# Four recurrent heads in one set of score groups, joint norms, gates ahead of the attentions, no transposes of empty causal blocks, and a planner without its shift table

## The chip, the cores and the metric

The kernel runs on one core of one Trainium2 chip. A core has TensorE (PE, 128 x 128 matrix engine, whose weight loads are shown as PEld), VectorE (DVE), ScalarE (ACT) and GpSimd (POOL), and queues that issue DMAs from SyncE (SP), ScalarE and GpSimd. The metric is device time in microseconds: the median of several executions.

## The reference

One layer of a hybrid decoder on x of 512 x 1024 in float32. Three groups read the same normed input and are merged by one output projection; a SwiGLU feed-forward layer follows. Cut to what the change touches:

```python
# A) latent attention, 4 heads, causal over blocks of 128 queries
q = (rmsnorm(c_q, q_a_norm) @ w_uq); kv = rmsnorm(c_kv, kv_a_norm) @ w_ukv
q = rmsnorm(q); k = rmsnorm(k); rope on 64 of 192 columns
p = softmax(where(kpos <= qpos, q @ k.T * scale, -inf));  o = p @ v
# B) HGRN2, 4 heads, one gated linear recurrence each
f = lb + (1 - lb) * sigmoid(f_raw); k = 1 - f; decay = exp of the cumulated log f
a[t, s] = sum_d q[t, d] * k[s, d] * decay(t, s, d)   for s <= t
o = a @ v + (carried state);  o = rmsnorm(o per head) * silu(g_raw)
# C) cross attention of 4 heads into 256 memory tokens, q and k rmsnormed
# then: x += concat(rmsnorm(A), B, rmsnorm(C)) @ w_out
#       x += (silu(h @ w_gate) * (h @ w_up)) @ w_down,  h = rmsnorm(x)
```

## The kernel before

**Arithmetic.** Every float32 operand of a large product is split into two parts, `hi` and `lo` (`split`: a cast on ScalarE, a subtraction on VectorE), and a product is three matmuls, hi·hi, hi·lo and lo·hi (`mm3`). Activations lie transposed: 128 features on the partitions, the 512 positions along the row. The feed-forward layer is a seven-product scheme (`fast`) and isn't touched.

**Order.** The program is first recorded. `run` (L244) then simulates the five engines with a price for each operation (`price`, L184), and always takes the ready operation with the least priority number; `issue` (L368) writes the instructions in that planned order, so nearly all of them carry line 388, and the matmuls of a `tiles` group (many small matmuls into column tiles of the PE array, one after the other) line 385. `rec.first(n)` gives a priority class. `NUDGE` (L242) is a table of 17 shifts of the priorities of stretches of the recording. Tiles come from rings (`BUFS`, L432): 3 PSUM banks for `mm`, 3 for `at`, 2 for `tr`; a tile waits until its ring has a free one.

**Start.** `WARM` matmuls on ones run while the first data come. ScalarE's queue issues five loads of `we` (two blocks of input weights that are needed first, `EARLY`, L402), SP's queue eight loads of x (`tm<-in_xT`), then the rest. x is split with its gain into `xh`, `xl`. The squares of x are summed (ScalarE squares, VectorE adds, `td`), `colsums` (L544) sums over the partitions with 32-wide column tiles against ones, `rsqrt_col` (L529) takes an inverse square root in ten small VectorE operations, and `spread` (L554) transposes its four columns to a 128 x 512 block, which ScalarE copies to `RX`. Each projection's bank (`mm`) is multiplied by `RX` on its way out (`td<-mm,RX`).

**Recurrence.** `hg_in` (L698) makes q, k and the gate of a head. `hg_levels` (L757) builds the causal matrix of two heads by doubling: at level m = 1, 2, ..., 64, pairs of blocks of m positions are combined. At each level a group of score matmuls (L385, `at<-y,tm`) reads the present q (`y`) and k (`tm`); for m up to 16 each head gives 16 parts of 32 x 32, spread over four column tiles; at m = 32 a head gives 8 parts; at m = 64 it gives 4 parts of 64 x 64, all in the lower column tile. `put` copies what a level has added under a mask (`cc<-lmask,at`), and `step_up` (L816) multiplies half of q and half of k by the totals of the neighbour block, in place, so that the next level's scores wait for it. Heads 0 and 1 go first, then heads 2 and 3. `hg_out` (L828) multiplies with the values and takes each head's norm by itself: a sum over partitions, an inverse root, four transposes.

**The rest.** `wide` projects the values of the recurrence (`wva` 320 columns, `wvb` 256). `lowrank` (L906) projects the compressed q and kv, each with a norm (`rcq`, `rckv`). In the attention, `softmax` makes weights `p` block by block (`p` is cleared beyond the diagonal), `weights_t` (L1062) transposes four 128 x 128 blocks of two query blocks, and `pv` (L743) multiplies with the values. `rope_t` (L1082) transposes a head's rotary part twice over into one 128 x 512 block. `hg_final` (L852) projects the output gate of a recurrent head and applies it; it is written after the latent attention. `group_norm` (L1072) norms a group's four heads jointly; that of the memory group stands right ahead of the last third of the output projection, on which the norm of the feed-forward layer rests.

Of the kernel before, what the change touches and what calls it, by code (L numbers as in the profile page):

```python
# [24 lines left out]
EPS = 1e-6  # L25
LEVELS = (1, 2, 4, 8, 16)
# [19 lines left out]
class Recorder:  # L46
# [137 lines left out]
    def price(self, o, outs, ins):  # L184
# [3 lines left out]
        if o.eng == "tensor":  # L188
            if o.name == "tiles":
                return 310 + 1.81 * sum(max(35, self._free(p[2])) for p in o.kw["parts"]) / len({self._rng(p[0])[2] for p in o.kw["parts"]})  # L190
# [50 lines left out]

    NUDGE = ((2868, 2885, -117), (1571, 1576, -1459), (2382, 2422, -477), (1732, 1734, 30), (826, 835, 186), (957, 1012, 3), (5620, 5660, 284), (3804, 3864, -113), (987, 1017, 110), (2666, 2693, -105), (2466, 2475, -61), (2533, 2540, 37), (2401, 2403, -37), (3367, 3411, -5), (3019, 3021, 346), (16, 18, 380), (2, 19, 3),)  # L242
# [158 lines left out]
WARM = 12  # L401
EARLY = {0: (1, "p"), 1: (2, "p"), 3: (2, "tc"), 5: (2, "tc"), 7: (1, "tc")}  # L402
XLAG = 0
X_ORDER = (0, 4, 1, 5, 2, 6, 3, 7)
# [8 lines left out]
def body(ctx, tc, t):  # L413
# [115 lines left out]
    def rsqrt_col(v, n):  # L529

        y = small(n)
        u = small(n)
        V.tensor_scalar(y.bitcast(I32), v.bitcast(I32), -0.5, float(0x5F3759DF), ALU.mult, ALU.add)
# [10 lines left out]
    def colsums(sqs, nblk=NB):  # L544
# [4 lines left out]
            (v[g:g + 32, i, b], sqs[i][:, b * P + g:b * P + g + 32], ones, (i, b) == ks[0], (i, b) == ks[-1])  # L549
            for i, b in ks for g in range(0, P, 32)  # L550
        ])
        return v[..., 0]
# [8 lines left out]
    def rms(sq, n):  # L561
        v = small(NB)
        V.tensor_scalar(v, colsum(sq, NB), 1.0 / n, EPS, ALU.mult, ALU.add)
# [16 lines left out]
    with rec.first(0):  # L580
# [5 lines left out]
        for k, (n, tag) in EARLY.items():  # L586
            w = ws[k] = sb(tag)[:, :2 * n * P + 8 * (k == 0)]
            A.dma_start(out=w, in_=t["we"][:, 2 * k * P + 8 * (k > 0):2 * (k + n) * P + 8])
# [3 lines left out]
        for k in range(KD):  # L592
# [5 lines left out]
            r = sb("tm")  # L598
            DMA.dma_start(out=r, in_=t["xT"][:, k * S:(k + 1) * S])
# [31 lines left out]
    early_tr[0] = False  # L631

# [65 lines left out]
    def hg_in(h):  # L698
        with rec.first(2):
            z, s_ = gated(5 + h)  # L700
            q = sb("tm")
# [3 lines left out]
            fg = sb("tm")  # L705
# [37 lines left out]
    def pv(v, h, pt, ns, y):  # L743
# [3 lines left out]
        for s in range(ns):  # L747
            mm3(o, cut(v[s], slice(None), hs), tuple(x[:, 2 * s:2 * s + 2, :].rearrange("p a b -> p (a b)") for x in pt), s == 0, s == ns - 1)
# [8 lines left out]
    def hg_levels(hs):  # L757

        N2 = range(len(hs))
        As = [sb("p", (P, NB, P)) for i in N2]  # L760
        C = sb("cc", (P, len(hs), NB, 32))
        old, hs = hs, [(sb("y"), k_, tot) for q, k_, tot in hs]

        def scores(sets):

            n = len(sets) * len(hs)
            o = ps_at()[:, 0:n * NB * 32].rearrange("p (n b t) -> p n b t", t=32, b=NB)
            ps_ = [(b, g) for b in range(NB) for g in range(0, P, 32)]
            all_ = [(i * len(hs) + j, h) for j in N2 for i, s in enumerate(sets) for h in (s[j],)]
            T.tiles(o, *[x for i, h in all_ for x in h[:2]], parts=[  # L770
# [722 lines left out]
```

## Time and profile before

| | us |
|---|---|
| median of 3 runs | 708.37 (707.99 to 708.49) |
| the profiled execution | 707.76 |
| its span, first to last instruction | 706.0 |
| TensorE busy | 697.1 (99%) |
| VectorE busy | 552.4 (78%) |
| ScalarE busy | 384.8 (55%) |
| GpSimd busy | 93.4 (13%) |

The granted TensorE clock of the span is 1.000. An instruction's duration in the trace runs from its start to its modelled end, and matmuls overlap: the distance from one start to the next is what a matmul takes of the engine. A part of a `tiles` group is two matmuls in the trace, and one in the planned order. Times are from the start of the span.

### The profile page before, as it was taken

How to read it: one execution, taken by the hardware profiler on the slowest of the kernel's cores; microseconds unless marked ns; L12 is line 12 of the kernel's file. 1: busy time of each engine (PE TensorE's matmuls, PEld its weight loads, DVE VectorE, ACT ScalarE, POOL GpSimd, SP SyncE). 2: the span in 40 equal slices, each digit the busy share in tenths (PEclk: the TensorE clock that was granted, in tenths of full speed). 3: DMA queues.
4: the chain of work that ended last, by engine and by line, in shares of the span. 5: the costliest groups of instructions: out<-in, count | busy, mean ns of one | idle time of the engine just before them, and what ended most of it. 6: DMA issues, size and time to landing. Idle time of an engine off the chain costs nothing.

```text
span 706.0 us, 13190 instructions
## 1 busy us (share of the span) xinstructions
PE 697.1 (99%) x4813; PEld 581.1 (82%) x4813; DVE 552.4 (78%) x1295; ACT 384.8 (55%) x740; POOL 93.4 (13%) x128
## 2 busy tenths in 40 slices
PE   8999999999999999999999999999999999999997
PEld 5898887787888888888788787888888899999885
DVE  5898879979978899987999969766549767448642
ACT  6653553547765686765767653645553465444320
POOL 0000100000000000000314333032113212310000
PEclk9999999999999999999999999999999999999999
DMA  8232132014511233215999999789868848941241
GB/s 285 78 95 89 64 120 66 32 62 143 185 61 61 75 94 115 77 31 161 266 250 244 221 235 229 203 175 229 190 136 187 165 124 197 218 86 30 72 145 60
DMA packets 47728, 98.05 MB, mean 139 GB/s; under 512 B 5424, under 2 KB 15536, under 8 KB 47664
## 3 DMA queue, kind: packets, MB, share of 16 engines
q1 hardware_dynamic: 33120, 73.10, 32.3%
q0 software_dynamic: 13824, 23.07, 20.5%
q10 hardware_dynamic: 720, 1.05, 0.4%
q8 instruction: 37, 0.61, 0.3%
q14 instruction: 27, 0.22, 0.1%
HBM read 95.11 MB, written 2.10 MB: 138 GB/s over the span
## 4 chain that ended last, share of the span: by engine, by line
PE 91%; DVE 5%; DMA 1%; ACT 1%; issue 1%; SPq 0%; DVEq 0%; ACTq 0%
PE mm L388 46%; PE at L388 21%; PE tr L388 21%; PE at L385 1%; DVE wl L388 1%; DVE y L388 1%; DMA tm<-in_xT 1%; DVE tm L388 1%; DVE td L388 1%; PE tr L385 1%; DMA wr<-in_wf 1%; DVE xl L388 0%; DVE hd L388 0%; DVE v L388 0%; ACT wh L388 0%
## 5 line engine op out<-in xcount | busy, mean ns | idle before, releaser
L388 ACT CAST wh<-wr 128x512 fp32r<-128x512 f32 (+2 forms) x136 | 80.7, 598 | 96.4 <-PE mm L388 49.8
L388 DVE TENSOR_TENSOR wl<-wr,wh 128x512 fp32r<-128x512 f32 (+2 forms) x148 | 96.5, 659 | 31.9 <-issue 12.2
L388 PE MATMUL mm<-xh,wh 128*128 128x512 f32 x248 | 98.1, 398 | 1.4 <-ACT xh L388 1.2
L388 PE MATMUL mm<-xh,wl 128*128 128x512 f32 x248 | 99.0, 399 | 0.4 <-DVE wl L388 0.4
L388 PE MATMUL mm<-xl,wh 128*128 128x512 f32 x248 | 98.7, 399 | 0.3 <-DVE xl L388 0.2
L388 DVE TENSOR_TENSOR wl<-y,wh 128x512 fp32r<-128x512 f32 (+1 forms) x84 | 53.3, 639 | 43.3 <-PE tr L388 17.3
L388 ACT CAST wh<-y 128x512 fp32r<-128x512 f32 (+1 forms) x81 | 46.7, 580 | 67.5 <-PE at L388 36.7
L388 DVE TENSOR_TENSOR wl<-mx,wh 128x512 fp32r<-128x512 f32 (+1 forms) x72 | 45.9, 646 | 28.8 <-PE tr L388 19.3
L388 PE MATMUL mm<-wh,hd 128*128 128x512 f32 (+2 forms) x188 | 63.9, 366 | 0.0
L388 ACT CAST wh<-mx 128x512 fp32r<-128x512 f32 (+1 forms) x67 | 39.2, 586 | 40.9 <-PE at L388 21.6
L388 PEld LDWEIGHTS mm<-xh,wh 128*128 128x128 f32 x248 | 46.5, 188 | 11.1 <-ACT xh L388 2.1
L388 PEld LDWEIGHTS mm<-xl,wh 128*128 128x128 f32 x248 | 46.6, 188 | 10.4 <-DVE xl L388 2.2
L388 PEld LDWEIGHTS mm<-xh,wl 128*128 128x128 f32 x248 | 46.7, 188 | 8.4 <-DVE wl L388 1.0
L388 PE MATMUL at<-wh,hd 128*128 128x512 f32 (+1 forms) x132 | 49.2, 375 | 0.0
L388 POOL DMA_DIRECT2D y<-in_wu x36 | 33.3, 983 | 95.8 <-DVE wl L388 76.3
L388 PE MATMUL tr<-xl,wh 128*128 128x512 f32 x112 | 43.8, 391 | 0.0
L388 PE MATMUL tr<-xh,wh 128*128 128x512 f32 x112 | 43.8, 391 | 0.0
L388 PE MATMUL tr<-xh,wl 128*128 128x512 f32 x112 | 43.7, 390 | 0.0
L388 PEld LDWEIGHTS mm<-wh,hd 128*128 128x128 f32 x188 | 34.5, 188 | 5.0 <-ACT wh L388 0.3
L388 PE MATMUL mm<-wl,hd 128*128 128x512 f32 (+2 forms) x100 | 37.0, 370 | 0.1
L388 PE MATMUL mm<-wh,v 128*128 128x512 f32 (+1 forms) x96 | 36.3, 378 | 0.0
L388 PE MATMUL at<-wh,v 128*128 128x512 f32 (+1 forms) x96 | 35.8, 375 | 0.0
(376 smaller groups left out, 1719.8 us busy)
## 6 DMA issues: line engine op xcount, KB each, us to landing
wr<-in_wf SPq DMA_DIRECT2D x19, 512.0 KB, 3.7
wr<-in_wd SPq DMA_DIRECT2D x16, 512.0 KB, 4.9
mx<-in_wg SPq DMA_DIRECT2D x24, 256.0 KB, 5.2
mx<-in_wu SPq DMA_DIRECT2D x24, 256.0 KB, 5.2
y<-in_wu POOLq DMA_DIRECT2D x24, 256.0 KB, 5.7
tm<-in_xT SPq DMA_DIRECT2D x16, 256.0 KB, 4.2
wr<-in_wt SPq DMA_DIRECT2D x8, 512.0 KB, 4.4
wr<-in_wo SPq DMA_DIRECT2D x8, 512.0 KB, 3.7
```

What stands on the lines that cost most here:

```text
L385: r = self.nc.tensor.matmul(get(a), lhsT=get(b), rhs=get(c), start=first, stop=last, skip_group_check=True)
L388: r = getattr(getattr(self.nc, o.eng), o.name)(*[get(a) for a in o.args], **{k: get(a) for k, a in o.kw.items()})
```

## The change

- `rsqrt_col` has eight small operations in place of ten (another first guess, one Newton step and one step of higher order; its input is scaled by the constant `RC`).
- `EARLY` and `WARM`: 10 warm matmuls in place of 12; three of the five loads of `we` stay on ScalarE's queue, two go to SP's, between the loads of x. `NUDGE` is gone, and the price of a `tiles` group is 270 + 2.1 per column in place of 310 + 1.81.
- `hg_in` is called for all four heads ahead of `wva` and `wvb`, q and the gate in halves of the rings `pth` and `ptl`. `hg_levels` takes four heads: each group of score parts holds all four (64 parts up to m = 16; from m = 32 on, heads 0 and 1 and heads 2 and 3 lie in different column tiles). Their matrices lie in the ring `tm`.
- `hg_out` takes no norm; `hg_norm` takes that of the four heads in one group of column sums and one inverse root over 16 columns. The two low-rank norms are joined in the same way, and stand ahead of `hg_out`.
- `hg_gate`, the projections of the output gates with their application, stands ahead of the latent attention; `hg_final` only splits.
- In the latent attention the block above the diagonal of each pair of query blocks isn't transposed: three transposes in place of four, and GpSimd clears that block of `pth` and `ptl` in place of `p`. `rope_t` takes two heads of q in one block.
- The memory group's norm sums the squares of three heads in one group and those of the fourth in a second one.

The core of the diff:

```diff
-            if o.name == "tiles":
-                return 310 + 1.81 * sum(...) / len({...})
+                return 270 + 2.1 * sum(...) / len({...})
-    NUDGE = ((2868, 2885, -117), (1571, 1576, -1459), ...
-        for a, b, d in self.NUDGE:
-            for o in ops[a:b]:
-                o.prio += d
-WARM = 12
-EARLY = {0: (1, "p"), 1: (2, "p"), 3: (2, "tc"), 5: (2, "tc"), 7: (1, "tc")}
+WARM = 10
+EARLY = {0: (1, "p"), 1: (1, "p"), 2: (2, "tc"), 4: (2, "tc"), 6: (2, "tc")}
...
-        for _ in range(3):
-            V.tensor_tensor(u, y, y, ALU.mult)
-            V.scalar_tensor_tensor(u, u, -0.5, v, ALU.mult, ALU.mult)
-            V.scalar_tensor_tensor(y, u, 1.5, y, ALU.add, ALU.mult)
+        V.tensor_tensor(u, y, y, ALU.mult)
+        V.scalar_tensor_tensor(u, u, -1.0, v, ALU.mult, ALU.mult)
+        V.scalar_tensor_tensor(y, u, 2.38924456, y, ALU.add, ALU.mult)
+        V.tensor_tensor(u, y, y, ALU.mult)
+        V.scalar_tensor_tensor(u, u, 0.703952253**2, v, ALU.mult, ALU.mult)
+        V.scalar_tensor_tensor(u, u, -10 / 3, u, ALU.add, ALU.mult)
+        V.scalar_tensor_tensor(y, u, 5.0, y, ALU.add, ALU.mult)
...
+                    (A if k < 4 else DMA).dma_start(out=w, in_=t["we"][...])
+            xin.append(sb("tm"))
+            with rec.first(-1):
+                DMA.dma_start(out=xin[k], in_=t["xT"][:, k * S:(k + 1) * S])
...
+        def scores(hs):
+            o = ps_at().rearrange("p (n b t) -> p n b t", t=32, b=NB)
+            ks = [(j, b) for j in range(HN) for b in range(NB)]
+            T.tiles(o, *[x for h in hs for x in h[:2]], parts=[
+                (o[g:g + 32, j, b], hs[j][1][:, b * P + g:b * P + g + 32], hs[j][0][:, b * P + g:b * P + g + 32], (j, b) == ks[0], (j, b) == ks[-1])
+                for j, b in ks for g in range(0, P, 32)
+            ])
...
+                w = min(m, 64)
+                T.tiles(o, *[x for h in hs for x in h[:2]], parts=[
+                    (o[i + s * m:i + (s + 1) * m, j, b], hs[2 * s + j][1][:, b * P + i:b * P + i + m], hs[2 * s + j][0][:, b * P + i + m:b * P + i + 2 * m], (j, b) == ks[0], (j, b) == ks[-1])
+                    for j, b in ks for i in at for s in range(2)
+                ])
...
-        R = spread(rms(sumsq([y], tag="tc"), P))
-        V.scalar_tensor_tensor(y, y, smc("g_hg", h), R, ALU.mult, ALU.mult)
+    def hg_norm(ys):
+        v = small(4 * NB)
+        V.tensor_scalar(v.rearrange("p (h b) -> p h b", b=NB), colsums([sumsq([y], tag=("tc", "td")[h % 2]) for h, y in enumerate(ys)]), RC / P, RC * EPS, ALU.mult, ALU.add)
+        r = rsqrt_col(v, 4 * NB)
+        for h, y in enumerate(ys):
+            V.scalar_tensor_tensor(y, y, smc("g_hg", h), spread(r[:, h * NB:(h + 1) * NB]), ALU.mult, ALU.mult)
...
-    qkf = [hg_in(0), hg_in(1)]
+    qkf = [hg_in(h) for h in range(4)]
...
-    for h, st in enumerate(hg_levels(qkf)):
-        yh.append(hg_out(h, *st))
-    qkf = [hg_in(2), hg_in(3)]
-    for h, st in enumerate(hg_levels(qkf)):
-        yh.append(hg_out(2 + h, *st))
+    qkt = hg_levels(qkf)
...
+    for h in range(4):
+        hg_gate(h, yh[h])
...
+            ends = causal and s == ns - 2
+            if ends:
+                for x in pt:
+                    G.memset(f(x)[:, 2 * s, :], 0.0)
-            for i in range(4):
+            for i in range(ends, 4):
...
-        R = spread(rms(sumsq(ys, tag="tc"), S))
+        n = 3 if late else 4
+        R = spread(rms(sumsq(ys[:n], tag="tc"), S, sumsq(ys[3:], tag="tc") if late else None))
...
-    group_norm(ys, 8, "g_mo", ("xh", "xl"))
+    group_norm(ys, 8, "g_mo", ("xh", "xl"), True)
```

**Where the order of instructions changes.** Three places follow; names are the program's with a running number, `A<-B,C` is an output and its inputs.

TensorE behind x's norm. `tr<-cst,rx` are the four transposes of `spread`, `mm` the banks of projections, `tr` with 320 columns those of `wva`. Before:

```order
L388 MATMUL tr_2165<-cst,rx 128x128 x4
L388 MATMUL mm_2089<-xl_2057,wh_2069 128x512
L388 MATMUL mm_2089<-xh_2042,wl_2093 128x512
L388 MATMUL tr_2173<-wh_2099,xh_1943 128x320
L388 MATMUL tr_2173<-wl_2145,xh_1943 128x320
L388 MATMUL tr_2173<-wh_2099,xl_1952 128x320
L388 MATMUL tr_2181<-wh_2099,xh_1943 128x320
L388 MATMUL tr_2181<-wl_2145,xh_1943 128x320
L388 MATMUL tr_2181<-wh_2099,xl_1952 128x320
L388 MATMUL tr_2173<-wh_2141,xh_1970 128x320
L388 MATMUL tr_2173<-wl_2175,xh_1970 128x320
L388 MATMUL tr_2173<-wh_2141,xl_1977 128x320
```

and of the changed kernel:

```order
L383 MATMUL mm_2048<-xh_2010,wh_2035 128x512
L383 MATMUL mm_2048<-xl_2020,wh_2035 128x512
L383 MATMUL tr_2126<-cst,rx 128x128 x4
L383 MATMUL mm_2048<-xh_2010,wl_2058 128x512
L383 MATMUL mm_2145<-xh_1901,wh_2052 128x512
L383 MATMUL mm_2145<-xl_1909,wh_2052 128x512
L383 MATMUL mm_2145<-xh_1901,wl_2071 128x512
L383 MATMUL mm_2145<-xh_1916,wh_2052 128x512
```

Before, two matmuls of an open bank and nine of `wva` stood between the transposes and the next projection's bank (`mm_2194`); now one matmul stands there, and then `mm_2145`, the next bank of the ring.

TensorE at level m = 2 of the recurrence (`at` is the group's bank, `y` and `tm` are q and k of a head, 16 parts each). Before, two heads:

```order
L388 MATMUL mm_2254<-wh_2289,xh_2037 128x320
L388 MATMUL mm_2254<-wl_2315,xh_2037 128x320
L385 MATMUL at_2452<-y_2307,tm_2268 32x32 x16
L385 MATMUL at_2452<-y_2328,tm_2310 32x32 x16
L388 MATMUL mm_2254<-wh_2289,xl_2050 128x320
L388 MATMUL mm_2264<-wh_2289,xh_2037 128x320
```

and of the changed kernel, four:

```order
L383 MATMUL mm_2428<-wh_2459,xl_1987 128x320
L380 MATMUL at_2694<-y_2257,tm_2226 32x32 x16
L380 MATMUL at_2694<-y_2296,tm_2263 32x32 x16
L380 MATMUL at_2694<-y_2379,tm_2371 32x32 x16
L380 MATMUL at_2694<-y_2558,tm_2477 32x32 x16
L383 MATMUL mm_2436<-wh_2459,xh_1976 128x320
L383 MATMUL mm_2436<-wl_2480,xh_1976 128x320
```

The group has twice as many parts, and stands among the matmuls of `wva` here too.

TensorE at the spread of the memory group's norm (`tr<-cst,sm`), ahead of the first bank that takes its results (`mm<-xh` with the number of a new `xh`). The changed kernel:

```order
L383 MATMUL mm_6218<-xh_5610,wl_6107 128x512
L383 MATMUL tr_6296<-cst,sm_6263 128x128 x4
L383 MATMUL mm_6218<-xh_5617,wh_6022 128x512
L383 MATMUL mm_6218<-xl_5632,wh_6022 128x512
L383 MATMUL mm_6218<-xh_5617,wl_6107 128x512
L383 MATMUL mm_6218<-xh_5643,wh_6022 128x512
L383 MATMUL mm_6218<-xl_5651,wh_6022 128x512
L383 MATMUL mm_6218<-xh_5643,wl_6107 128x512
L383 MATMUL mm_6322<-xh_6314,wh_6094 128x512
L383 MATMUL mm_6324<-xh_6314,wh_6146 128x512
```

Before, the spread was followed by 18 matmuls of an open bank (`mm_6197`) ahead of the first such bank (`mm_6457`); its end there:

```order
L388 MATMUL mm_6197<-xh_5802,wl_6307 128x512
L388 MATMUL mm_6197<-xh_5828,wh_6246 128x512
L388 MATMUL mm_6197<-xl_5839,wh_6246 128x512
L388 MATMUL mm_6197<-xh_5828,wl_6307 128x512
L388 MATMUL mm_6457<-xh_6425,wh_6302 128x512
L388 MATMUL mm_6457<-xl_6438,wh_6302 128x512
```

Now six stand there, and the first matmuls behind them take one `xh` into three banks.

## Rows read from the trace of the kernel before

**Rows 1.** The page of the profile, part 1: busy time, share of the span and number of instructions of each engine.

```profile
PE 697.1 (99%) x4813; PEld 581.1 (82%) x4813; DVE 552.4 (78%) x1295; ACT 384.8 (55%) x740; POOL 93.4 (13%) x128
```

**Rows 2.** The page, part 4, the chain of work that ended last: shares of the span by engine.

```profile
PE 91%; DVE 5%; DMA 1%; ACT 1%; issue 1%; SPq 0%; DVEq 0%; ACTq 0%
```

**Rows 3.** The waits of TensorE, the whole span: who waits for whom: us in total, times, the longest.

```profile
PE mm L388 <- ACT xh L388: 1.2, 1, 1.2
PE at L388 <- DVE ptl L388: 0.2, 1, 0.2
```

**Rows 4.** Timeline of TensorE around a score group of 64 parts (the diagonal and level 1 of heads 2 and 3), which begins in the second row here and lies ahead of the third. Columns: start us, us, engine, line, operation, out<-in, count, and idle time before with what ended it.

```profile
103.65 0.39 PE L388 MATMUL mm<-xh,wh 128*128 128x512 f32 x1
103.97 0.46 PE L385 MATMUL at<-tm,tm 128*32 128x32 f32 x32
...
105.54 0.39 PE L388 MATMUL mm<-xh,wl 128*128 128x512 f32 x1
```

**Rows 5.** The same around a score group of 32 parts (one level of two heads; a part counts as two matmuls).

```profile
108.03 0.39 PE L388 MATMUL mm<-xl,wh 128*128 128x512 f32 x1
...
108.71 0.39 PE L388 MATMUL mm<-xl,wh 128*128 128x512 f32 x1
109.03 0.76 PE L385 MATMUL at<-y,tm 128*32 128x32 f32 x64
...
110.06 0.39 PE L388 MATMUL mm<-xh,wh 128*128 128x512 f32 x1
```

**Rows 6.** The same around the groups of level 32 (16 parts, two column tiles of 32) and level 64 (8 parts, one column tile of 64) of heads 2 and 3.

```profile
125.45 0.39 PE L388 MATMUL mm<-xl,wh 128*128 128x512 f32 x1
...
126.90 0.40 PE L388 MATMUL mm<-xh,wh 128*128 128x512 f32 x1
...
128.99 0.40 PE L388 MATMUL mm<-xh,wh 128*128 128x512 f32 x1
129.32 1.15 PE L385 MATMUL at<-y,tm 128*64 128x64 f32 x16
...
130.73 0.40 PE L388 MATMUL mm<-xh,wl 128*128 128x512 f32 x1
```

**Rows 7.** Timeline of TensorE around a column-sum group of 16 parts (one norm).

```profile
84.81 0.39 PE L388 MATMUL mm<-xh,wh 128*128 128x512 f32 x1
85.12 0.43 PE L385 MATMUL tr<-ones,tc 128*32 128x2 f32 x32
...
85.82 0.39 PE L388 MATMUL mm<-xh,wl 128*128 128x512 f32 x1
```

**Rows 8.** The same around a column-sum group of 32 parts (two squares in one group).

```profile
149.32 0.40 PE L388 MATMUL mm<-hd,wh 128*128 128x512 f32 x1
149.65 0.71 PE L385 MATMUL tr<-ones,td 128*32 128x2 f32 x64
...
150.62 0.60 PE L388 MATMUL tr<-cst,sm 128*128 128x128 f32 x4
```

**Rows 9.** Timeline of the first 8 us: TensorE, ScalarE and the DMA issues of ScalarE's queue (ACTq).

```profile
1.22 5.49 PE L388 MATMUL tr<-ones_r 128*128 128x512 f32 x12 [1.22 <-DVE ones_r L388]
...
4.32 2.49 ACTq L388 DMA_DIRECT2D tc<-in_we  x2
...
6.85 0.40 ACT L388 CAST wh<-p 128x256 fp32r<-128x256 f32 x1 [3.69 <-DMA p<-in_we]
...
7.93 0.73 PE L388 MATMUL mm<-xh,wh 128*128 128x512 f32 x2 [1.22 <-ACT xh L388]
```

**Rows 10.** Busy time by stretch: us, then busy us and instructions of TensorE, of its weight loads, of VectorE, ScalarE and GpSimd, the granted clock, the DMA share and GB/s.

```profile
7.28:21.60 14.32, 13.40 (x55) 9.85 (x56) 13.81 (x24) 13.05 (x24) 1.05 (x2) 1.00 0.62 236
```

**Rows 11.** Timeline of all engines from the column sum of x's norm (22.04) to the first matmul behind the copies of it (28.09).

```profile
22.04 0.43 PE L385 MATMUL tr<-ones,td 128*32 128x2 f32 x32
...
25.48 0.39 PE L388 MATMUL mm<-xh,wh 128*128 128x512 f32 x1
...
25.74 0.62 PE L388 MATMUL tr<-cst,rx 128*128 128x128 f32 x4
...
26.40 0.59 ACT L388 COPY RX<-tr 128x512 f32<-128x512 f32 x1 [2.54 <-PE tr L388]
26.43 0.40 PE L388 MATMUL mm<-xh,wl 128*128 128x512 f32 x1
...
27.35 1.28 DVE L388 TENSOR_TENSOR td<-mm,RX 128x512 f32<-128x512 f32 x2
...
28.09 0.50 PE L388 MATMUL mm<-xh,wh 128*128 128x512 f32 x1
```

**Rows 12.** Timeline of VectorE in a level of heads 0 and 1: the masked copy and the multiplications of a step up.

```profile
45.50 0.45 DVE L388 COPY_PREDICATED cc<-lmask,at 128x256 f32<-128x256 uint8 x1
45.84 0.42 DVE L388 TENSOR_TENSOR y<-y,tm 128x256 f32<-128x256 f32 x1
46.17 0.42 DVE L388 TENSOR_TENSOR tm<-tm,tm 128x256 f32<-128x256 f32 x1
```

**Rows 13.** Timeline of VectorE and TensorE behind the spread of the memory group's norm.

```profile
330.19 1.40 DVE L388 SCALAR_TENSOR_TENSOR y<-y,smv,tr 128x512 f32<-128x512 f32 x2
...
348.00 0.39 PE L388 MATMUL at<-wh,hd 128*128 128x512 f32 x1
...
349.54 0.50 PE L388 MATMUL mm<-xh,wl 128*128 128x512 f32 x1 [0.36 <-DVE wl L388]
```

More of the change, by code (lines that the diff above doesn't have):

```diff
@@ L189, in price @@
             if o.name == "tiles":
-                return 310 + 1.81 * sum(max(35, self._free(p[2])) for p in o.kw["parts"]) / len({self._rng(p[0])[2] for p in o.kw["parts"]})
+                return 270 + 2.1 * sum(max(35, self._free(p[2])) for p in o.kw["parts"]) / len({self._rng(p[0])[2] for p in o.kw["parts"]})
             if o.name == "transpose":
@@ L548, in colsums @@
         T.tiles(o, ones, *sqs, parts=[
-            (v[g:g + 32, i, b], sqs[i][:, b * P + g:b * P + g + 32], ones, (i, b) == ks[0], (i, b) == ks[-1])
+            (v[g:g + 32, i, b], sqs[i][:, b * P + g:b * P + g + 32], ones, (i, b) == ks[0], (i, b) == ks[-1] and more is None)
             for i, b in ks for g in range(0, P, 32)
         ])
+        if more is not None:
+            T.tiles(o, ones, more, parts=[
+                (v[g:g + 32, 0, b], more[:, b * P + g:b * P + g + 32], ones, False, b == nblk - 1)
+                for b in range(nblk) for g in range(0, P, 32)
+            ])
         return v[..., 0]
@@ L585, in body @@
         ws = {}
-        for k, (n, tag) in EARLY.items():
-            w = ws[k] = sb(tag)[:, :2 * n * P + 8 * (k == 0)]
-            A.dma_start(out=w, in_=t["we"][:, 2 * k * P + 8 * (k > 0):2 * (k + n) * P + 8])
+        xin = []
+        for k in range(KD):
+            if k in EARLY:
+                n, tag = EARLY[k]
+                w = ws[k] = sb(tag)[:, :2 * n * P + 8 * (k == 0)]
+                with rec.first(-1):
+                    (A if k < 4 else DMA).dma_start(out=w, in_=t["we"][:, 2 * k * P + 8 * (k > 0):2 * (k + n) * P + 8])
+            xin.append(sb("tm"))
+            with rec.first(-1):
+                DMA.dma_start(out=xin[k], in_=t["xT"][:, k * S:(k + 1) * S])
         gain = ws[0][:, 2 * P:]
@@ L631, in body @@
     early_tr[0] = False
+    normed = rec.last("scalar")
     rec.held = len(rec.ops) - 2
@@ L747, in pv @@
         for s in range(ns):
-            mm3(o, cut(v[s], slice(None), hs), tuple(x[:, 2 * s:2 * s + 2, :].rearrange("p a b -> p (a b)") for x in pt), s == 0, s == ns - 1)
+            at = slice(2 * s, 2 * s + 2)
+            if causal and s >= ns - 2:
+                at = slice(2 * s + 1, 2 * s + 3) if s == ns - 2 else slice(2 * s - 2, 2 * s + 2, 3)
+            mm3(o.rearrange("p (a b) -> p a b", b=P), cut(v[s], slice(None), hs), tuple(x[:, at, :] for x in pt), s == 0, s == ns - 1)
         A.copy(y, o)
@@ L791, in hg_levels @@
                 if m == 16:
-                    for j in N2:
+                    for j in range(HN):
                         for g in range(0, P, 32):
                             A.copy(As[j][g:g + 32, :, g:g + 32], C[g:g + 32, j])
-            elif m == 32:
-                o = ps_at()[:, 0:len(hs) * NB * 32].rearrange("p (n b t) -> p n b t", t=32, b=NB)
+            else:
+                w = min(m, 64)
+                o = ps_at()[:, 0:2 * NB * w].rearrange("p (n b t) -> p n b t", t=w, b=NB)
+                at = range(0, P, 2 * m)
+                ks = [(j, b) for j in range(2) for b in range(NB)]
@@ L862, in body @@
     hv, yh = [], []
-    qkf = [hg_in(0), hg_in(1)]
+    spots = [x[:, i * S:(i + 1) * S] for tag in ("pth", "ptl") * 2 for x in (sb(tag, (P, 8, P), F32R).rearrange("p a b -> p (a b)"),) for i in range(2)]
+    qkf = [hg_in(h) for h in range(4)]
     kr = cp.tile([P, NB, 64], F32, name="kr")
@@ L920, in body @@
     cq, cq_sq = lowrank(0, 3, "g_qa")
[L921 to L935 removed]
+    ckv, ckv_sq = lowrank(3, 2, "g_kva", "tc")
+    with rec.first(0):
+        o = colsums([cq_sq, ckv_sq])
+        v = small(2 * NB)
+        for i, n in enumerate((384, 256)):
+            V.scalar_tensor_tensor(v[:, i * NB:(i + 1) * NB], o[:, i], RC / n, rx2, ALU.mult, ALU.mult)
+        V.tensor_scalar(v, v, RC * EPS, None, ALU.add)
+        rlow = cp.tile([P, 2, NB], F32, name="rlow")
+        V.tensor_tensor(rlow, rsqrt_col(v, 2 * NB).rearrange("p (i b) -> p i b", b=NB), rx.unsqueeze(1).broadcast_to([P, 2, NB]), ALU.mult)
+    rcq, rckv = rlow[:, 0], rlow[:, 1]
+    for h, st in enumerate(qkt):
+        yh.append(hg_out(h, *st))
+    hg_norm(yh)
     def sq_heads(dst, src):
@@ L1080, in group_norm, with rope_t @@
             mix[i0 + i] = (hi, lo)
-    def rope_t(src, h):
+    def rope_t(src):
         o = ps_tr()
```

139 lines of the change are left out of this document (55 added, 84 removed).

## The prediction

> **What bounds the kernel now.** I read the page's busy times first, then the chain that ended last, then TensorE's waits, and then timelines at the places that the change touches. TensorE is busy for 697.1 of 706.0 us and VectorE for 552.4 [rows 1]; the chain is TensorE for 91% [rows 2]. Its waits are single events: 1.2 us for the first `xh`, 0.2 for a `ptl` [rows 3]. So the time is the length of TensorE's list of instructions, with a few holes. A change gains what it takes off that list, and loses where it leaves the list without something to do; what it takes off VectorE or ScalarE counts only at such holes. The unit of the list is a matmul of 512 columns: three starts lie 0.68 us apart (108.03 to 108.71), 0.227 us each [rows 5]. The cost of a group is the distance from the start of the matmul ahead of it to the start of the second matmul behind it, less two such steps (0.454).
>
> **Score groups.** 64 parts: 105.54 - 103.65 - 0.454 = 1.44 us [rows 4]. 32 parts: 110.06 - 108.71 - 0.454 = 0.90 [rows 5]. So 32 parts more cost 0.54, and 0.36 is the price of a group as such. Level 32: 126.90 - 125.45 - 0.454 = 1.00; level 64: 130.73 - 128.99 - 0.454 = 1.29 [rows 6]. Before, each pair of heads has one group of 64 parts (diagonal and level 1), four of 32, and one each at levels 32 and 64: 2 x (1.44 + 4 x 0.90 + 1.00 + 1.29) = 14.66. Now, for all four heads, six groups have 64 parts (the diagonal, and levels 1 to 16): 8.64. Level 32 has 32 parts on four column tiles, as an ordinary level of two heads had: 0.90. Level 64 has twice the parts on two column tiles where it had one; I take 1.29, that is, full overlap of the two tiles. Sum 10.83, so **-3.8**. Does overlap hold? A part costs (0.90 - 0.36) / 32 = 0.017 us on four tiles, and (1.00 - 0.36) / 16 = 0.040 on two [rows 5, 6]: half the tiles, over twice the price, so 32-wide tiles overlap. For 64-wide tiles no row shows it. Without any gain from the added tiles level 32 would cost 0.36 + 2 x 0.64 = 1.64 and level 64 0.36 + 2 x 0.93 = 2.22: 1.67 more, and the term falls to -2.1. I take the former, because the 32-wide rows are the nearest.
>
> The Trainium skill, "TensorEngine Tiling (Array Packing)", section "Key Properties", says that different tiles can load weights and multiply in parallel, and that a change of the tiling mode drains the engine. The 32-wide rows agree with the first and the 0.36 us for a group with the second; by it the term is -3.8, and it shows no figure of its own for two 64-wide tiles.
>
> **Column sums.** 16 parts: 85.82 - 84.81 - 0.454 = 0.56 [rows 7]; 32 parts: 150.62 - 149.32 - 0.454 = 0.85 [rows 8]; by that slope 64 parts cost 1.43. Four head norms of 0.56 become one of 1.43: -0.81. Two low-rank norms become one of 0.85: -0.27. The memory group's norm now has two groups in place of one: +0.56. Sum **-0.5**.
>
> **Transposes.** In the latent attention 3 of 4 remain in the last group of each pair of query blocks, 2 groups a head: -8. `rope_t` of q is made for two heads at once, two calls of 4 transposes less: -8. Four transposes cost 26.43 - 25.48 - 0.454 = 0.50 us [rows 11], 0.124 each: 16 x 0.124 = **-2.0**. The added clearing of `pth` and `ptl` is on GpSimd, which is busy for 13% [rows 1]; uncovered it would cost one such clearing at each of 8 places, and the clearing of `p` that it replaces had the same cover.
>
> **Start.** Before, ScalarE issues two more loads from 4.32 to 6.81, then casts at 6.85, and the first real matmul starts at 7.93, 1.08 behind the cast; its 12 warm matmuls take 5.49, 0.457 each [rows 9]. Now three loads are issued there, and ten warm matmuls end at 1.22 + 4.57 = 5.8: the first matmul can come 2.1 earlier. But between its first subtraction at 7.28 and the last addition of squares VectorE is busy for 13.81 of 14.32 us [rows 10]; it sets when the column sum (22.04, rows 11) comes, and it now has one more piece of such work there (0.64, by 1.28 for two, rows 11). So 1.5 of the 2.1 remain. The two small operations less in the inverse root save 0.4 of its chain. Against it stands the first place of the order: before, two matmuls and nine of `wva` covered the copy to `RX` and the multiplication that frees the next bank, from 25.74 to 28.09 [rows 11]. The same chain without VectorE's subtraction in between is some 2.1 us (transposes to copy 0.66, copy 0.6, a wait of 0.1, multiplication 0.64, a wait of 0.1), and what now stands there is the transposes and one matmul, 0.7: TensorE is idle for 1.4. Together -1.5 - 0.4 + 1.4 = **-0.5**. Bounds: -2.1, where VectorE keeps pace and the bank is free in time; and +2.3, where the first ten matmuls run at the warm ones' step (10 x 0.23) and nothing else is gained.
>
> **Levels of four heads.** Between one level's scores and the next, VectorE has a masked copy (0.34 us for two heads, by 45.50 to 45.84, so 0.68) and eight multiplications of 0.33 [rows 12]: 3.3 us, with two heads 1.7. TensorE's cover is the `wva` matmuls (second place of the order) and then the low-rank projections. I count shortages of 0.1 to 0.3 at most levels, and 0.6 at `hg_out`, against the small holes that the present levels have: **0**, with -1 and +4 as ends.
>
> **The memory group's norm.** Six matmuls (1.36) follow the spread in place of 18 (4.1). VectorE needs three multiplications of 0.70 [rows 13] in a row, an addition and the first `xl` of 0.64 each: some 3.5 us until `xl` can be used, while TensorE has those six and three more on `xh` (0.68). So about 1.5 us of new idle time. In the present trace TensorE loses 349.54 - 348.00 - 3 x 0.227 = 0.86 shortly behind this place, waiting for a `wl` of an overfull VectorE [rows 13]; that queue drains while TensorE now stands, so I let it go. Net **+0.5** (0 to +1.7).
>
> **Moved without a price.** The gates (96 matmuls, 21.8 us) ran beside the attentions as something to do; their loads and the activations move with them, and the same queues carry them. In the attentions the key and value projections of the memory, its queries and the output projection remain for that. The table of shifts had single stalls to smooth; what takes its place is bounded by the ends above.
>
> **Sum.** -3.8 - 0.5 - 2.0 - 0.5 + 0 + 0.5 = -6.3 on 707.76, the time of the profiled execution: 701.5. The median of the runs shown lies 0.61 above that execution: **702.1 us**.
>
> **Rivals.**
> - Levels bound by VectorE (slower): if `wva` and the low-rank matmuls are used up or not ready, each of 7 levels waits for the second pair's four multiplications, 4 x 0.33 = 1.3. That is +9.2: 711.3. It decides from (709.8 - 702.1) / 7 = 1.1 us a level. For it: 3.3 us of VectorE behind each group. Against it: the order shows matmuls on both sides of every group, and VectorE has 22% of the span free [rows 1].
> - The start gives nothing, and the idle time at `RX` stays: 702.1 + 0.5 + 1.4 = 704.0. For it: VectorE's row of 96% [rows 10].
> - The groups don't pack as meant (the change doesn't do what it says): 702.1 + 1.7 = 703.8.
> - The latent attention lacks the gates' matmuls: 16 blocks of softmax, each with a wait as the `ptl` one of 0.2 [rows 3], +3.2: 705.3. For it: that wait exists already. Against it: only one of them does.
> - The start gives all of 2.1 and `RX` is no bar: 700.5.
>
> **How the numbers follow.** Chances: forecast 0.45, start nothing 0.15, no packing 0.10, attention short of work 0.10, full start 0.12, slower 0.08. The range of 699.5 to 706.8 takes the first five with the ends of their terms (-2.0 of start and levels below, +4 of the levels above), and leaves out the slower rival and as much again at its two ends. A measurement here tells 0.2% (1.4 us) from no change: below 706.95 is faster, above 709.79 slower. Faster 0.86 (all of the forecast, the two starts and the packing but 0.02, and 0.06 of the attention), same 0.06, slower 0.08.
>
> **What would show it.** Right: six groups of 64 parts at about 1.44, level 64 at 1.3, TensorE's busy time some 6 us less, the first real matmul near 5.8 to 6.5, an idle time of about 1.4 ahead of the multiplied bank behind `RX`, and one of about 1.5 behind the last spread. Wrong: level 64 at 2.2; waits of TensorE for `at<-y` inputs (`y`, `tm`) of over 1 us at the levels; waits for `ptl` or `p` in each block of the latent attention; or a busy time that falls while the span doesn't.

## The result, and the profile after

| | before | after |
|---|---|---|
| median of 20 runs, us | 708.47 (707.76 to 709.25) | 711.09 (709.29 to 714.49) |
| the profiled execution | 707.76 | 711.22 |
| its span | 706.0 | 709.4 |
| TensorE busy | 697.1 | 693.0 |

The ratio of the changed kernel to the one before is 1.0039 [1.0031, 1.0048]: slower, by 2.6 us in the medians, where 702.1 was forecast. TensorE's busy time fell by 4.1 us and the span rose by 3.4. So TensorE was left standing, or ran slowly, for longer than the change takes off its list.

The page's busy times, and TensorE's waits (who waits for whom: us in total, times, longest), which answer to [rows 1, 3]; the chain is TensorE for 90% here [rows 2]:

```profile
PE 693.0 (98%) x4827; PEld 580.6 (82%) x4827; DVE 548.9 (77%) x1231; ACT 374.8 (53%) x720; POOL 95.3 (13%) x140
```

```profile
PE at L380 <- issue: 4.8, 2, 3.2
PE mm L383 <- DVE td L383: 1.5, 1, 1.5
...
PE at L380 <- DVE tm L383: 1.1, 2, 0.8
PE tr L383 <- DVE ptl L383: 1.0, 2, 0.8
```

The first line is new in kind: at two groups of score parts TensorE stood for 4.8 us and waited for nothing that the profile shows ("issue"). Timeline of TensorE at these two places (start, duration, out<-in, count, idle time before and what ended it), the first at level 1, the second at level 4:

```profile
60.17 0.86 PE L380 MATMUL at<-y,tm 128*32 128x32 f32 x76
64.25 0.66 PE L380 MATMUL at<-y,tm 128*32 128x32 f32 x52 [3.21 <-issue]
64.83 0.64 PE L383 MATMUL tr<-wh,xl 128*128 128x320 f32 x1
65.27 0.47 PE L383 MATMUL mm<-wh,xh 128*128 128x320 f32 x1
65.53 0.47 PE L383 MATMUL mm<-wl,xh 128*128 128x320 f32 x1
...
68.34 0.31 PE L383 MATMUL mm<-wh,xh 128*128 128x320 f32 x1
68.49 0.31 PE L383 MATMUL mm<-wl,xh 128*128 128x320 f32 x1
...
81.73 1.13 PE L380 MATMUL at<-y,tm 128*32 128x32 f32 x108
84.45 0.38 PE L380 MATMUL at<-y,tm 128*32 128x32 f32 x20 [1.59 <-issue]
```

A group of 64 parts is 128 matmuls. It stops in its middle, after 76 or 108 of them, at a weight load that waits for no semaphore: of the groups' own waits for operands, the first group's only one stands some 20 matmuls behind the stop, and the second group's two, 45 and 13 matmuls ahead of it, had been passed. The long stop has an echo: matmuls of 320 columns then start 0.26 us apart (65.27 to 65.53), and later 0.15 (68.34 to 68.49). From 64.83 to 68.34 there are 13 steps in 3.51 us, where 13 of 0.1465 make 1.90: 1.6 us more. The windows view shows the granted clock beside it (us, then busy us and instructions of PE, PEld, DVE, ACT, POOL, the clock, DMA share, GB/s):

```profile
60.00:80.00 20.00, 16.57 (x340) 15.63 (x339) 13.96 (x37) 5.08 (x10) 0.82 (x4) 0.91 0.22 75
```

From 80 to 100 us it is 1.00 again. These two places cost 4.8 + 1.6 = 6.4 us. A group that isn't cut, of all four heads, answers to [rows 4]: 98.81 - 96.93 - 0.454 = 1.43.

```profile
96.93 0.39 PE L383 MATMUL mm<-xh,wh 128*128 128x512 f32 x1
97.25 1.30 PE L380 MATMUL at<-y,tm 128*32 128x32 f32 x128
...
98.81 0.39 PE L383 MATMUL mm<-xh,wl 128*128 128x512 f32 x1
```

Levels 32 and 64, which answer to [rows 6]:

```profile
105.39 0.39 PE L383 MATMUL mm<-xl,wh 128*128 128x512 f32 x1
...
106.98 0.45 PE L380 MATMUL at<-y,tm 128*32 128x32 f32 x30 [0.78 <-DVE tm L383]
...
107.70 0.39 PE L383 MATMUL mm<-xh,wh 128*128 128x512 f32 x1
...
113.85 0.39 PE L383 MATMUL mm<-xh,wh 128*128 128x512 f32 x1
...
114.81 1.43 PE L380 MATMUL at<-y,tm 128*64 128x64 f32 x30 [0.32 <-DVE tm L383]
...
116.50 0.39 PE L383 MATMUL mm<-xh,wl 128*128 128x512 f32 x1
```

Here the stops name VectorE's `tm` of the second pair of heads: 0.78 and 0.32. Without them level 32 costs 107.70 - 105.39 - 0.454 - 0.78 = 1.08, and level 64 116.50 - 113.85 - 0.454 - 0.32 = 1.88.

The column sums of the two low-rank norms (32 parts) and of the four heads (64) now lie side by side; they answer to [rows 7, 8]. Together 146.87 - (144.21 + 0.227) - 0.454 = 1.98.

```profile
144.21 0.61 PE L383 MATMUL mm<-hd,wh 128*128 128x512 f32 x2
...
146.87 0.64 PE L383 MATMUL mm<-hd,wh 128*128 128x512 f32 x2
```

The start (first 8 us, x's column sum, the copies to `RX`), which answers to [rows 9, 11]:

```profile
5.83 1.05 PE L383 MATMUL mm<-xh,wh 128*128 128x512 f32 x2
...
20.39 0.43 PE L380 MATMUL tr<-ones,td 128*32 128x2 f32 x32
...
24.21 0.48 PE L383 MATMUL mm<-xh,wl 128*128 128x512 f32 x1
26.15 0.50 PE L383 MATMUL mm<-xh,wh 128*128 128x512 f32 x1 [1.46 <-DVE td L383]
```

And two places that no step of the prediction had, in the feed-forward layer, which the change doesn't touch:

```profile
369.83 0.39 PE L383 MATMUL at<-wh,hd 128*128 128x512 f32 x1
370.79 0.50 PE L383 MATMUL mm<-wh,v 128*128 128x512 f32 x1 [0.58 <-ACT v L383]
...
439.23 0.39 PE L383 MATMUL at<-wh,hd 128*128 128x512 f32 x1
440.38 0.44 PE L383 MATMUL tr<-cst,ptl 128*128 128x128 f32 x2 [0.76 <-DVE ptl L383]
```

A start that comes later than its step of 0.227 is a hole: 0.73 at 369.83, 0.92 at 439.23. With those at 371.83 (0.29), 426.83 (0.41), 440.38 (0.43) and 441.05 (0.36) the layer has 3.1 us of them.

### The profile page after: what moved, and what is told of

Same layout as the page of the kernel before. It is cut to its first block, busy times and chain, and to the rows that moved or that the text cites. A ratio compares the mean times of both kernels' runs of the same rounds, so it can differ in the third digit from the quotient of the medians.

```text
span 709.4 us, 13185 instructions
## 1 busy us (share of the span) xinstructions
PE 693.0 (98%) x4827; PEld 580.6 (82%) x4827; DVE 548.9 (77%) x1231; ACT 374.8 (53%) x720; POOL 95.3 (13%) x140
## 4 chain that ended last, share of the span: by engine, by line
PE 90%; DVE 6%; ACT 2%; issue 1%; DMA 1%; ACTq 0%; DVEq 0%
PE mm L383 46%; PE at L383 21%; PE tr L383 21%; PE at L380 1%; DVE wl L383 1%; DMA tc<-in_we 1%; DVE tm L383 1%; PE tr L380 1%; DVE td L383 1%; DVE y L383 1%; ACT wh L383 1%; DVE ptl L383 0%; DVE hd L383 0%; DVE qr L383 0%; ACT tm L383 0%
```

## The experiments

**Theories.** A: the stops belong to TensorE's stream of instructions. It comes in blocks, and where short instructions use a block up too quickly, the engine stands at the border until the next has come. B: they belong to these groups, through an operand, a PSUM bank or VectorE. By A their place moves with the count of instructions ahead; by B it stays with the group. For A speaks the count: a matmul is two instructions of TensorE's stream (weight load and matmul), so 128 matmuls are 256. Counted along the program's order, semaphore instructions included, the two stops lie at the instructions 961 and 1730, which leave 193 and 194 by 256, the same place in a block but for one instruction. And the page lists a queue that carries instructions: 0.62 MB in 38 packets, 16 KB each.

```profile
q8 instruction: 38, 0.62, 0.4%
```

The DMA view of three stretches around the first stop has one such packet, between 61.7 and 62.1, over 2.1 us ahead of the resumption at 64.25, right behind the last packets of a data load (`wvb`, 512 KB). (Row: queue, packets, MB, share of 16 engines, of the stretch 61.7 to 62.1.)

```profile
q8 instruction: 1, 0.02, 14.5%
```

The Trainium skill, "Runtime: NRT & Kernel Launch", section "Instruction fetch mechanics", states the blocks: an engine's instructions come 256 at a time, 16 KiB, the next fetched while the present one is executed, and crossing a border is mostly hidden, since instructions go out more slowly than they come in. The count and the packets agree with the blocks, and "mostly" holds: in the traces of the twelve kernels of this document 432 of 444 borders pass without a stop. The other 12, with up to 3.21 us, don't agree with the reason.

**after_shift23: the count moved by 23 matmuls.** Ahead of the first real matmul, 12 small parts (24 matmuls in the trace) take the place of one warm matmul; the rest of the order is as it was.

```diff
+        warm = 0
         ...
+            if o.eng == "tensor":
+                warm += 1
+                if warm <= 1:
+                    continue
+                if warm == WARM + 1:
+                    q, w = self.pad
+                    for i in range(12):
+                        g = i % 4 * 32
+                        r = self.nc.tensor.matmul(get(q)[g:g + 32, 0:2], lhsT=w[:, 0:32], rhs=w[:, 0:2], ...)
+                        self.tc.keep_in_program_order(r)
```

> The changed kernel with 12 tiny parts (24 matmuls and 24 weight loads) in place of one of the ten warm matmuls; the order of everything else is the same. Theory A (TensorE's instructions come in blocks of 256, one block is fetched when the one before it is used up, and a score group of 64 parts eats a whole block in 1.3 us): the stalls sit at fixed numbers of instructions, so the one in the level-1 group comes 23 matmuls earlier, behind 53 of its 128 matmuls in place of 76, again some 3 us; the one in the level-4 group moves from 108 to 85 and shrinks from 1.6 to under 0.8. Time 709.5 to 711. Theory B (a stall from the data: a bank, a buffer or VectorE): the level-1 group stops again behind 76 matmuls, since all that it waits for is where it was.

Measured: 717.64 (715.79 to 719.00), ratio 1.0122 [1.0100, 1.0145]. Timeline of TensorE (the first row of each pair is the group's first piece):

```profile
61.14 0.66 PE L391 MATMUL at<-y,tm 128*32 128x32 f32 x53
64.85 1.13 PE L391 MATMUL at<-y,tm 128*32 128x32 f32 x75 [3.04 <-issue]
...
82.46 0.93 PE L391 MATMUL at<-y,tm 128*32 128x32 f32 x85
85.34 0.72 PE L391 MATMUL at<-y,tm 128*32 128x32 f32 x43 [1.95 <-issue]
...
151.71 0.29 PE L391 MATMUL tr<-ones,td 128*32 128x2 f32 x8 [2.59 <-issue]
```

76 became 53 and 108 became 85: both stops moved by 23 matmuls, as A has it to the matmul, and B falls. The size was missed: 717.64 for the 709.5 to 711 of A. The stop at level 4 didn't shrink, and a third one came, 2.59 us long, after 120 matmuls of the four heads' column sums, which follow the 64 of the low-rank norms directly; behind it lies a slow stretch (granted clock 0.66 from 148 to 158). The place is known, then, and this run alone doesn't tell what sets the length.

**after_shift88: the same by 88.** `warm <= 2`, and 45 parts.

> The changed kernel with 45 tiny parts (90 matmuls and their weight loads) in place of two warm matmuls; all else in the same order. Theory A: the block borders now fall at the end of the diagonal group (behind 121 of its 128 matmuls) and behind 116 of the level-1 group, each with a stall of 1.4 to 3.3 us, and behind 110 of the level-8 group (0.3 to 2.1) and in the joint column sums of the heads (2.4 to 4.2); none in the level-4 group. In all 5.5 to 14 us of stalls against 4.8 in the changed kernel: 713 to 719. Theory B: 711, stalls where they were.

Measured: 709.14 (707.45 to 710.30), ratio 1.0008 [0.9998, 1.0018]. Only one stop is left, after 116 matmuls of level 1's group; 76 - 88 + 128 = 116. That place is A's, but its sum, 713 to 719, is missed by 4 us: the other forecast stops (at the diagonal, at level 8 and in the column sums) didn't come. Behind it the matmuls keep their step of 0.15. By the same count borders also lie after 88 matmuls of level 2 and 20 of level 4, and those groups run whole.

```profile
61.10 1.20 PE L391 MATMUL at<-y,tm 128*32 128x32 f32 x116
64.54 0.32 PE L391 MATMUL at<-y,tm 128*32 128x32 f32 x12 [2.25 <-issue]
...
65.04 0.30 PE L394 MATMUL mm<-wh,xh 128*128 128x320 f32 x1
65.19 0.31 PE L394 MATMUL mm<-wl,xh 128*128 128x320 f32 x1
```

Nothing of the work differs from after_shift23 but 66 small matmuls and one warm one, and the time differs by 8.5 us.

**before_shift29: a border in a group of the kernel before.** The same edit there with `warm <= 1` and 15 parts.

> The kernel before with 15 tiny parts (30 matmuls and their weight loads) in place of one warm matmul; all else in the same order. Theory A: a block border now falls behind 127 of the 128 matmuls of the first group of 64 parts (diagonal and level 1 of heads 0 and 1), 1.4 us behind the border before it less a few matmuls: a stall of 2.2 to 4.0 us there, which the kernel before doesn't have; 710.5 to 713. Theory B: 708.4, no such stall, since this kernel's groups and data are as they were.

Measured: 707.80 (707.61 to 708.59), ratio 0.9997 [0.9987, 1.0006], no "issue" row in TensorE's waits: the time is B's 708.4, and A's stall of 2.2 to 4.0 us didn't come. By the count borders lie at both ends of the first 128 matmuls, some 1.1 us apart, after 44 of a level's 64 matmuls and after 68 of the 128 of heads 2 and 3; the kernel before has such borders too. So a border within a group doesn't stop the engine by itself, nor does a border shortly ahead of it. The changed kernel's two borders, 81 matmuls into the diagonal (from 57.97) and 76 into level 1 (from 60.17), lie some 2.2 us apart, and there it stops.

**after_spread_old: the diagonal's group taken apart.** It is issued as four groups of 16 parts, with other work between them; with it 11 small parts.

```diff
-        def scores(hs):
+        def scores(hs, parts=1):
...
+            n = HN // parts
+            for s in range(0, HN, n):
+                T.tiles(o, *[x for h in hs[s:s + n] for x in h[:2]], parts=[
...
+                    for j, b in ks if s <= j < s + n for g in range(0, P, 32)
...
-        V.tensor_tensor(C, scores(old), ...)
+        V.tensor_tensor(C, scores(old, 4), ...)
```

> The changed kernel with the diagonal's score group (64 parts, right ahead of the level-1 group) issued as four groups of 16 parts, one as each head becomes ready, and 11 tiny parts (22 matmuls) in place of one warm matmul, so that by count no block of 256 instructions of TensorE is used up in under 3.6 us. Theory A (blocks of instructions): no stall inside any score group or column sum; three more groups cost 3 x 0.36 = 1.1, the stalls and the slow matmuls behind them (6.5) go: 705 to 706.5. Theory B (data, banks): the level-1 group waits as before, 710 to 712.

Measured: 708.44 (708.25 to 709.04), ratio 1.0000 [0.9990, 1.0009]. Level 1's group runs whole; the stop at level 4 is 1.16. The gain is 2.7 us on the changed kernel, where 5 or 6 were expected; level 4's stop is left, and two new waits of 0.3 for ScalarE's `tm`. The time lies between the ranges of A (705 to 706.5) and B (710 to 712).

```profile
63.19 1.30 PE L391 MATMUL at<-y,tm 128*32 128x32 f32 x128
...
81.80 0.63 PE L391 MATMUL at<-y,tm 128*32 128x32 f32 x49 [1.16 <-issue]
```

**after_no_wvb_load: is the block late because of a data load?** The pieces of `wvb` are taken from `RX`, so its loads of 512 KB, one of which is in flight at the first stop of the changed kernel, are gone (and half of the recurrence's values are other numbers). At the second stop a load of `wf` is in flight there.

```diff
-                raw = load(src[...], ...)
+                if n == 256:
+                    raw = RX.unsqueeze(1).broadcast_to([P, 2, S])
+                else:
+                    raw = load(src[...], ...)
```

> The changed kernel with the second half of the recurrence's value weights not loaded: the matmuls take the 128 x 512 block RX in their place, so half of the values are wrong. TensorE's order is the same. Theory A1 (the packet of instructions waits behind the load that is in flight at that time): the stall behind 76 matmuls of the level-1 group falls from 3.2 to 1.0 to 1.8 us, and its packet comes 1 to 1.5 us behind the border ahead of it in place of 3.3. Theory A2 (the fetch takes this long by itself): 3 us as before. The level-4 stall has another load beside it and should stay at 1.6.

Measured: 710.08 (708.60 to 710.67), ratio 1.0019 [1.0008, 1.0029].

```profile
64.47 0.65 PE L380 MATMUL at<-y,tm 128*32 128x32 f32 x52 [2.47 <-issue]
...
83.61 0.38 PE L380 MATMUL at<-y,tm 128*32 128x32 f32 x20 [0.50 <-issue]
```

The stops shrink from 3.21 and 1.59 to 2.47 and 0.50, where A1 had 1.0 to 1.8 and 1.6, and A2 3 and 1.6. But the edit doesn't take the load away from the first stop: the next loads come earlier, and between 59 and 62.5 us a load of `wf` is now in flight (row of the issue: count, KB, us to landing).

```profile
q1 hardware_dynamic: 144, 0.52, 46.1%
...
wr<-in_wf SPq DMA_DIRECT2D x1, 512.0 KB, 3.5
```

It is gone from the second stop instead: between 78.5 and 82.4 us the DMA view has one packet, that of the instructions.

```profile
q8 instruction: 1, 0.02, 1.8%
```

So without a load the stop is 0.50 us. No run takes the loads away from the first stop.

**The packets in all twelve traces.** All 12 stops of the traces lie behind 192 or 193 instructions from a multiple of 256. Counted at that remainder, each trace has 37 borders that go with the packets one by one, in order: 444 in all. At each of the 12, TensorE reaches the border before the packet starts or less than 1.9 us behind its start, and goes on 2.2 to 2.9 us behind its start. At the other 432 it comes 2.19 us or more behind that start, and there is no stop. So a stop is as long as the packet is late for its border. That has two parts: a block that is used up quickly (before after_shift23's third stop in 1.1 us, with the packet 1.0 us behind the border before) and a packet that starts late (before its second stop 6.7 us behind that border, with a block that lasted 6.8). Late packets go with data loads: in 11 of the 12 cases 119 to 141 packets of loads began in the 2 us ahead of the instruction packet, and in 10 of them it started only as the last of these ended. The 12th is the stop of 0.50.

**after_shift88_one_norm: the memory group's norm in one group of sums again**, on top of after_shift88.

```diff
-    group_norm(ys, 8, "g_mo", ("xh", "xl"), True)
+    group_norm(ys, 8, "g_mo", ("xh", "xl"))
```

> The run with 88 matmuls of padding (709.1), with the memory group's norm as it was before the change: the four squares summed in one group. Theory 1 (the second group lets the norm come earlier, and is worth its 0.56 us of TensorE): the waits at the first banks behind the norm grow from 1.4 to over 2.5 us; 709.5 to 711. Theory 2 (it only costs): 708 to 708.8. What the planner makes of the feed-forward layer behind it may move it by 1 us either way.

Measured: 708.16 (705.97 to 708.47), ratio 0.9991 [0.9981, 1.0000]; against after_shift88 about 1 us, at the edge of both intervals. The holes behind the spread are (331.97 - 330.55 - 0.227) + (333.18 - 331.97 - 0.681) = 1.72, against 1.45 with the split: by these rows the split saves 0.3 us there and costs a group (0.56 by [rows 7]), so it doesn't pay; the time, within theory 2's 708 to 708.8, agrees, but doesn't show it clear of noise.

```profile
330.55 0.40 PE L394 MATMUL mm<-xh,wl 128*128 128x512 f32 x1
331.97 0.98 PE L394 MATMUL mm<-xh,wh 128*128 128x512 f32 x3 [1.02 <-ACT xh L394]
333.18 0.50 PE L394 MATMUL mm<-xl,wh 128*128 128x512 f32 x1 [0.23 <-DVE xl L394]
```

**before_no_table: what was the table of shifts worth?** In the kernel before, `NUDGE = ()`.

> The kernel before without its table of 17 priority shifts. Theory 1 (the waits of the changed kernel in the feed-forward layer, at 370, 427 and 440 us, some 3 us, come from the missing table): 710.5 to 712, with such waits at those places. Theory 2 (they come from the moved work ahead of them): within 0.7 us of 708.4.

Measured: 711.64 (711.41 to 711.77), ratio 1.0046 [1.0031, 1.0061]: 3.3 us, in single waits of TensorE (the first row is the whole span, the second 120 to 340 us).

```profile
PE mm L388 <- ACT xh L388: 4.0, 3, 2.3
...
PE mm L388 <- ACT xh L388: 3.5, 2, 2.3
```

The time is theory 1's, the places aren't: the two waits end at 283.13 and 337.53, and at 370, 427 and 440 us this kernel has none of over 0.2. So the table's worth is measured here, and not that its absence made the changed kernel's waits.

**after_table: a table for the changed kernel.** Five shifts, made for its own order.

```diff
+    NUDGE = ((3636, 3654, 317), (3049, 3054, -887), (5586, 5646, -135), (45, 55, 531), (8, 40, 754))
...
+        for a, b, d in self.NUDGE:
+            for o in ops[a:b]:
+                o.prio += d
```

> The changed kernel with a table of its own of five shifts of priority; the order changes at the start (what stands behind the transposes of x's norm) and in the feed-forward layer from some 350 us on, nothing in the recurrence. Theory 1 (the waits for the first bank behind RX, 1.7 us, and at 370, 427 and 440 us, 3.1 us, come from a planner whose order nobody corrected, and not from the moved work): most of these 4.8 us go: 706.5 to 708.5, with the two stalls of the score groups where they were, behind 76 and 108 matmuls. Theory 2 (the moved work leaves too little to stand there): waits of the same sum come back elsewhere, over 710.

Measured: 708.68 (707.08 to 712.66), ratio 1.0007 [0.9991, 1.0023]. The largest wait of TensorE between 340 and 470 us is now this:

```profile
PE mm L388 <- ACT wh L388: 0.7, 1, 0.7
```

The stops of the instruction stream are the same two (4.7 us in all), and the hole behind `RX` has gone to an earlier place (1.48 at 10.65, for `xh`). By the same reckoning as above, the holes between 340 and 470 us fall from 3.1 to 1.2. So some 2.4 us of the median come back from the waits alone, just beyond theory 1's 706.5 to 708.5. The profiled execution is one of the longer ones (711.64).

**combined_234 and combined_72: both causes taken away.** The diagonal in four groups, one group of sums for the memory norm, a table of 16 shifts, and small parts that move the borders: 59 with `warm <= 2`, and 19 with `warm <= 1`.

> The changed kernel with the diagonal's scores in four groups of 16 parts, one group for the memory norm's squares, a table of 16 shifts made for this recording, and padding (59 tiny parts in place of two warm matmuls) at which by count no block of 256 instructions is used up in under 3.9 us. Theory A with theory 1: stalls and slow matmuls -6.5, waits -4.8, one column-sum group -0.56, three more score groups +1.1: 711.1 - 10.8 = 700 to 702. If the blocks are not the cause (theory B): 705 or more. If the table only moves the waits: 704 to 706.

> The same kernel with 19 tiny parts in place of two warm matmuls: by count the shortest block is used up in 3.4 us (among the matmuls of the value weights, behind the level-1 group), the next in 3.8 (level-2 group). Theory A: at most one stall of under 1.5 us, and within 1.5 us of the other padding. Theory B: the same time as the other padding.

Measured: 702.64 (702.51 to 702.90), ratio 0.9918 [0.9903, 0.9932], and 702.59 (701.81 to 703.14), ratio 0.9916 [0.9901, 0.9930]. Both beat both kernels; the first lies 0.6 above the 700 to 702 of A with theory 1, and below the 704 to 706 of a table that only moves the waits. No "issue" wait is left in either; TensorE's largest waits in combined_72, behind that for its first operand:

```profile
PE mm L399 <- ACT xh L399: 1.2, 1, 1.2
PE at L399 <- DVE wl L399: 0.8, 1, 0.8
```

Which of the four edits brings how much isn't taken apart here. The two tried alone, the diagonal in four groups (2.7, with its padding) and a table of five shifts (2.4), make 5.1 of the 8.5 us.

## Why the prediction was wrong

It said 702.1 and the time is 711.1. One of its signs of being wrong came true, a busy time that falls (4.1 us, for some 6) while the span doesn't. The slower rival's 711.3 is met by luck: it counted 9.2 us of waits for VectorE at the levels, and these are 1.1. By its own steps:

- **Score groups, -3.8.** The price of a whole group of 64 parts was right, 1.43 for 1.44. Level 32 costs 1.08 for 0.90, and level 64 1.88 for 1.29: the two 64-wide tiles overlap in part only, between the forecast and the "no packing" end of 2.22. Six groups of 1.43 with these make 11.54 and a gain of 3.1. The rival of no packing holds for 0.59 of the 0.93 us that it had at level 64.
- **Column sums, -0.5.** Right, and 0.3 on the safe side: the two joint groups cost 1.98 together, where the slope gave 0.85 + 1.43 = 2.28. The second group of the memory norm is the part that doesn't pay (after_shift88_one_norm).
- **Start, -0.5.** The mechanism and nearly the sizes hold: the first matmul at 5.83 for 5.8, the column sum 1.65 earlier for 1.5, and 26.15 - 24.21 - 0.227 = 1.71 of idle time behind `RX` for 1.4.
- **The memory group's norm, about 1.5 of idle time.** 0.27 + 0.82 + 0.36 = 1.45, behind 334.39, 334.89 and 336.16; and the wait for `wl` of [rows 13] is gone.
- **Transposes, -2.0.** No run takes them alone.
- **"Levels of four heads: 0, with -1 and +4".** This step failed. It, and the slower rival, asked only whether VectorE would be late: VectorE's waits at the levels are 1.1 us, near the forecast. The other 6.4 us are the stops of TensorE's own stream and the slow matmuls behind them, a resource that no step named. The step took a 64-part group's price from groups that stood far apart, and the change puts the diagonal 2.2 us ahead of level 1. Shown: the stops' place follows the count of instructions, and their length the start of the instruction packet. Without any stop, and with most of the holes closed, the time is 702.6; that agrees with the sum for the work, but doesn't show it, since that kernel has three groups more, one group of sums less and a table of its own.
- **"Moved without a price."** This failed as well: 3.1 us of holes in the feed-forward layer. The table was worth 3.3 us in the kernel before, and a short one gives 2.4 back in the changed kernel. To bound its loss by the ends of other terms was an error. Whether the missing table made these holes, or the moved work, stays open, since the kernel before, without its table, has them at other places; the table's loss and the holes are of one size.
- **The range.** With the ends that it names, 702.1 + 4 = 706.1 is its upper end and not 706.8, and the lower one, 699.5, takes 2.6 off and not 2.0. The measured time is outside either way.

The gains in the sum stood on work; the losses came as holes, 6.4 + 3.1 + 1.1. With the groups (0.7), the sums (-0.3) and `RX` (0.3) these errors come to 11.3, and the profiled execution lies 711.22 - 701.5 = 9.7 above the sum. So 1.6 us of gains are not placed; the small holes of the kernel before, for which the prediction had no term, are a likely place, not a shown one.

What stays open is why a packet starts when it does. after_shift23's 1.95 at level 4 came with a border some 7 us earlier, and its packet started 6.7 us behind that border, as a load's last packets ended. In the twelve traces a packet starts anywhere from 4.9 us ahead of the border before its own to 6.7 us behind it. That a load holds it back is read from their order in time; a run that moves the loads alone wasn't made.

## What to carry to other kernels

Count instructions, not only columns and microseconds: where a matrix engine gets hundreds of tiny matmuls in a row, look where the borders of 256 instructions fall and which data loads are in flight there, keep such groups apart, and move the borders by a few small instructions where a stop sits in a group. A padding can also do harm: 24 small matmuls in place of a warm one cost 6.5 us in after_shift23. When a schedule was smoothed by hand, an edit to the order has to be priced with the smoothing gone (here 3.3 us), or timed only after it has been smoothed again. And a wait that names nothing, at an instruction that waits for no semaphore, is a finding in itself.

## What the hardware showed that I had not expected

- TensorE stops at borders of its instruction stream for 0.5 to 3.2 us on straight code, where 128 small matmuls take 1.3 us. It goes on 2.2 to 2.9 us behind the start of the packet that brings the next block.
- Behind a stop of 3.21, 3.04, 2.83 or 2.47 us matmuls of 320 columns run at 0.266 us a step in place of 0.1465 for some 2 to 3 us (the lower one of the clock's two levels, 1.2 GHz); behind stops of 2.46 (after_shift88_one_norm), 2.25 and 1.59 us they don't. The length alone doesn't decide: behind 1.95 (after_shift23) and 1.87 us (after_table) the granted clock of the next 4 us is 0.57 as well.
- Two 64-wide column tiles overlap only in part: 1.88 - 0.36 = 1.52 us for 32 matmuls, 0.048 each, where one such tile had (1.29 - 0.36) / 16 = 0.058; full overlap would be 0.029.
